# Sixty-four bytes of SBUF moved among the operand tiles of a float32 decoder trunk

## The chip, the cores and the metric

The kernel runs as one program on one core of a Trainium2 chip. The metric is the device time of one execution in microseconds (us); 842.84 us is the median of three runs of the kernel before.

## The reference

Two decoder layers over 256 tokens of width 1024, all in float32. Layer 0 mixes tokens by latent attention (MLA: low-rank query and key/value projections, rotary key), layer 1 by dilated window attention (three head groups). Each mixer is followed by a SwiGLU feed-forward net of inner width 2816 and by a gated per-layer embedding, with norms around each part:

```python
h = h + rms_norm(y, g[1])
h = h + rms_norm(swiglu(rms_norm(h, g[2]), ffn_w_in[i], ffn_w_out[i]), g[3])
h = h + (p[i] @ ple_w_proj[i]) * jax.nn.sigmoid(h @ ple_w_gate[i])
```

Here `y` is the mixer's output. Nearly all the arithmetic is the products with the weights, which are read once, 136 MB in all.

## The kernel before, in words

**Split products.** Every product with a weight is made from two-part splits in the type float32r. A value v is split into a high part (ScalarE copies v into a float32r tile, L219 for weights) and a low part (VectorE subtracts, L220). `mm3` (L291) then issues three matmuls into the same PSUM columns through `mm` (L288, the matmul itself is L289): weight high by x high, weight high by x low, weight low by x high. Each matmul is preceded by the load of its own stationary operand (a LDWEIGHTS, the engine PEld), which for one matmul runs while the matmul before it still streams. In a row such as `psin<-xh,wh 128*128 128x256` the moving operand (256 columns, 1024 bytes in each partition) is `xh`, the stationary one (128 columns, 512 bytes) is `wh`.

**Kinds of split product.** With the weight as stationary operand: x by w (`xh`, `xl`: all projections of the residual or of the attention output), u by w (`uh`, `ul`: the down projection `down`, L890), c by w (`ckvh`, `ckvl`, `cqh`, `cql`: the low-rank MLA projections) and p by w (`ph`, `pl`: the embedding, in `post_norm`). With the weight as moving operand: v of layer 1 (`v_chunk`, L1013, 384 columns, stationary `xh`, `xl`) and v of MLA (L650 to L657, 512 columns, stationary `ckvh`, `ckvl`).

**Order of the work.** The program is one written-out list for each engine. The feed-forward net goes block by block (L901 to L909): `half(f, 0)` and `half(f, 1)` are 24 matmuls x by w each into one PSUM bank, then `down(f - 3)` is 24 matmuls u by w over four banks, three matmuls at a time. The blocks f = 3 to 21 stand back to back in TensorE's list, 19 of them in each layer. In `square_matmul` (L431) and at the start of the net (L853 to L860) the outputs alternate after each three matmuls. In layer 1's mixer (L1107 to L1149) the six 24-matmul tiles of a head pair (`qk_tile`, L1007) have the attention of the pair before woven between them: scores with 64 rows, transposes, and products of probabilities with v. Eight head pairs make 1152 matmuls x by w.

**Weights.** `Stream` (L175) loads weights into three `raw` tiles of 8 KB per partition through the queue of SyncE, splits them into seven `wh` and seven `wl` tiles of 4 KB, and prepares as far ahead as free tiles allow.

**Addresses.** A pool hands out SBUF in the order in which tags are first asked for, in steps of 32 bytes; a tag with several buffers takes them side by side. The pool `main` begins with `cst` and `h`; then come, by the order of first use, `tbl` (two buffers of 32 bytes, the target of `table`, L298, that has ScalarE change its function table), `raw`, `xh`, `xl`, `wh`, `wl`, `acc` and small tiles. The pools of the stages lie behind it, each from the same byte 150464: `mla`, then `ffn` of layer 0, `dil`, and `ffn` of layer 1. All columns and chunks that the split products take begin at multiples of 512 bytes in their tiles, so one number for a tile, its address modulo 512, holds for each of its matmuls. In the program before:

| tiles | address of the first | modulo 512 |
|---|---|---|
| `tbl` (2 of 32 bytes) | 28160 | 0 |
| `raw` (3 of 8192) | 28224 | 64 |
| `xh`, `xl` (2 each of 8192) | 52800, 69184 | 64 |
| `wh`, `wl` (7 each of 4096) | 85568, 114240 | 64 |
| `ckvh`, `ckvl`, `cqh`, `cql` | 151552 to 158720 | 0 |
| `ph`, `pl`, both layers | 160704, 162752 | 448 |
| `uh`, `ul`, layer 0 (5 each of 1024) | 193024, 198144 | 0 |
| `uh`, `ul`, layer 1 | 177088, 182208 | 448 |

The `u` tiles of the two layers differ because layer 0's pool also holds the small tiles of the bias tables (L814 to L822).

Of the kernel before, what the change touches and what calls it, by code (L numbers as in the profile page):

```python
# [13 lines left out]
AF = mybir.ActivationFunctionType  # L14
# [246 lines left out]
def trunk(ctx: ExitStack, tc: tile.TileContext, tags, widths, wts, xT, pT, positions, consts,  # L261
# [7 lines left out]
    def nm(s):  # L269
        uid[0] += 1  # L270
        return f"{s}_{uid[0]}"

    def sb(tag, shape, dt=F32, bufs=1, pool=None):
        return (pool or main).tile(shape, dt, tag=tag, bufs=bufs, name=nm(tag))
# [10 lines left out]
    V, A, G, PE = nc.vector, nc.scalar, nc.gpsimd, nc.tensor  # L285
# [9 lines left out]

    px = fp = None

    def table(func, src):  # L298

        A.activation(sb("tbl", [128, 1], bufs=2), src, func)  # L300


    mla = ExitStack()
# [8 lines left out]
    def gain(i, n, k):  # L312
        c = C_G + (i * 4 + n) * 8 + k
        return cst[:, c:c + 1]


    def new_x():
        return sb("xh", [128, KT, T], F32R, bufs=2), sb("xl", [128, KT, T], F32R, bufs=2)
# [11 lines left out]

    zero = sb("zero", [128, 1], pool=mp)
    V.memset(zero, 0.0)
    table(AF.Sin, zero)

    idle = sb("ang", [128, T], pool=mp)
    V.memset(idle, 0.0)
# [13 lines left out]
    def ordered(ap):  # L350

        return ap.rearrange("p (i c) -> p c i", c=2)

    def blocks(ap):
        return ap.rearrange("p (c i) -> p c i", c=2)

    x = new_x()
    for k in range(KT):
        g = gain(0, 0, k)
        A.activation(ordered(x[0][:, k]), blocks(h[:, k]), AF.Copy, scale=g)  # L360
        V.scalar_tensor_tensor(ordered(x[1][:, k]), blocks(h[:, k]), g, ordered(x[0][:, k]).bitcast(F32),
                               op0=ALU.mult, op1=ALU.subtract)
        if k in (1, 3):
            ws.prep()
# [84 lines left out]
    def post_norm(i, n, acc, dst, proj, o0, x, g_next, sq_next, freed, ahead=0, extra=None):  # L449
# [11 lines left out]
        for k in range(KT):  # L461
# [11 lines left out]
            if k % 2 and k // 2 < len(freed):  # L473
                ws.hold(freed[k // 2], a, v)
        table(AF.Sigmoid, x[0][:, KT - 1, 0:1].bitcast(F32))
        if sq_next is not None:
            for k in range(KT):
# [112 lines left out]
    V.scalar_tensor_tensor(sin, sin, 2.0, cos, op0=ALU.mult, op1=ALU.mult)  # L590
    V.tensor_scalar(cos, kf, 1.0, None, op0=ALU.add)
    table(AF.Exp, cos[:, 0, 0:1])
    rep = sb("csr", [128, 2, 2, 128], pool=mp)
    V.tensor_copy(rep.rearrange("p a t (r f) -> p (a t) r f", f=16),
# [27 lines left out]
    for c in range(2):  # L622
        ch = ws.next("uk")
        for o in range(4):
# [12 lines left out]
            if o % 2 == 1:  # L637
                src = bu[-1].t.rearrange("p (o t) -> p o t", o=2)
# [163 lines left out]
    def sublayers(i, ot, done):  # L802
# [2 lines left out]
        ffn = ExitStack()  # L805
        fp = ffn.enter_context(tc.tile_pool(name=nm("ffn"), bufs=1))
        proj = sb("proj", [128, KT, T], pool=fp)
        pf = sb("pf", [128, 2, T], pool=fp)
        nc.gpsimd.dma_start(pf, pT[i])
        px = (sb("ph", [128, 2, T], F32R, pool=fp), sb("pl", [128, 2, T], F32R, pool=fp))  # L810
# [155 lines left out]

    mla.close()
    sublayers(0, ot, to_next)

    dil = ExitStack()  # L970
# [181 lines left out]
    def store(k):  # L1152
        nc.sync.dma_start(out[k * 128:(k + 1) * 128, :], h[:, k])

    sublayers(1, ot, store)
    assert ws.cur == len(widths)

# [72 lines left out]
```

## Time and profile before

| | |
|---|---|
| median of 3 runs | 842.84 us (842.48 to 843.18) |
| the profiled execution's own time | 842.93 us |
| its span (first to last instruction) | 841.2 us |
| TensorE busy | 827.2 us, 6780 matmuls |
| VectorE busy | 582.9 us |
| ScalarE busy | 456.7 us |
| DMA | 143.04 MB, 170 GB/s on average |

Matmuls overlap in the pipeline: a row's duration (some 0.28 us) is longer than the distance to the next start (some 0.12 us), and the distance between starts is what a matmul costs. A start in the timeline is given to 0.01 us, so distances are read over many matmuls.

### The profile page before, as it was taken

The numbers are of one execution on the slowest core, as the hardware profiler recorded it, in microseconds if no ns is written. First come the engines' busy times: TensorE is split into PE (matmuls) and PEld (weight loads), VectorE is DVE, ScalarE is ACT, GpSimd is POOL, SyncE is SP. The second block draws the span as 40 slices with busy tenths as digits, with TensorE's granted clock in tenths as the row PEclk, the third lists the DMA queues.
The fourth block names the chain that finished last, engine by engine and source line by source line (L and its number), as shares of the span: only waits on it lengthen the run. The fifth ranks groups of instructions, "written<-read, shape, count | busy, mean of one in ns | idle before, by whom it ended". The sixth has DMA issues, their size and how long they took to land.

```text
span 841.2 us, 16363 instructions
## 1 busy us (share of the span) xinstructions
PE 827.2 (98%) x6780; PEld 803.5 (96%) x6780; DVE 582.9 (69%) x1001; ACT 456.7 (54%) x782; POOL 63.8 (8%) x73
## 2 busy tenths in 40 slices
PE   8988999999999999999999999999999999999998
PEld 7976999999999999999999999999999999999997
DVE  6888478666666679695775775776578666666675
ACT  6748675444444477564554564565574444444462
POOL 3013220000000005100000000000210000000000
PEclk9999999999999999999999999999999999999999
DMA  7651336545545534755455455445426554554511
GB/s 254 212 219 51 122 102 219 202 181 201 186 172 194 200 104 151 275 175 192 147 177 182 155 170 182 163 141 198 136 82 253 194 189 168 196 188 167 197 51 51
DMA packets 23482, 143.04 MB, mean 170 GB/s; under 512 B 3071, under 2 KB 4175, under 8 KB 9200
## 3 DMA queue, kind: packets, MB, share of 16 engines
q1 hardware_dynamic: 21584, 135.98, 45.9%
q0 software_dynamic: 1824, 6.03, 2.8%
q8 instruction: 53, 0.87, 0.4%
q14 instruction: 21, 0.17, 0.1%
HBM read 140.86 MB, written 1.13 MB: 169 GB/s over the span
## 4 chain that ended last, share of the span: by engine, by line
PE 88%; DVE 4%; ACT 3%; DMA 2%; issue 1%; POOL 0%; SPq 0%; DVEq 0%; ACTq 0%
PE psin L289 40%; PE pspt L289 19%; PE psB L289 6%; PE psA L289 6%; PE psC L289 6%; PE psD L289 6%; PE psD L1092 2%; PE pspt L1075 2%; DVE wl L220 2%; DMA raw<-in_wts 1%; DMA h<-in_xT 1%; ACT mp L743 1%; ACT wh L219 1%; PE psin L771 0%; PE pspt L758 0%
## 5 line engine op out<-in xcount | busy, mean ns | idle before, releaser
L220 DVE TENSOR_TENSOR wl<-raw,wh 128x1024 fp32r<-128x1024 f32 (+1 forms) x265 | 315.6, 1197 | 160.8 <-ACT wh L219 160.0
L219 ACT ACTIVATE wh<-raw 128x1024 fp32r<-128x1024 f32 (+1 forms) x265 | 269.0, 1023 | 270.1 <-PE psin L289 115.6
L289 PE MATMUL psin<-xh,wh 128*128 128x256 f32 x768 | 220.1, 287 | 0.0
L289 PE MATMUL psin<-xh,wl 128*128 128x256 f32 x768 | 217.2, 283 | 0.0
L289 PE MATMUL psin<-xl,wh 128*128 128x256 f32 x768 | 217.1, 283 | 0.0
L289 PEld LDWEIGHTS psin<-xh,wh 128*128 128x128 f32 x768 | 146.8, 191 | 1.9 <-ACT rb L466 0.2
L289 PEld LDWEIGHTS psin<-xl,wh 128*128 128x128 f32 x768 | 146.9, 191 | 0.0
L289 PEld LDWEIGHTS psin<-xh,wl 128*128 128x128 f32 x768 | 146.9, 191 | 0.0
L289 PE MATMUL pspt<-xh,wl 128*128 128x256 f32 x440 | 124.8, 284 | 1.8 <-DVE wl L220 1.8
L289 PE MATMUL pspt<-xh,wh 128*128 128x256 f32 x440 | 125.1, 284 | 0.7 <-ACT wh L219 0.7
L289 PE MATMUL pspt<-xl,wh 128*128 128x256 f32 x440 | 124.6, 283 | 0.4 <-DVE xl L327 0.4
L289 PEld LDWEIGHTS pspt<-xh,wl 128*128 128x128 f32 x440 | 84.2, 191 | 2.4 <-DVE wl L220 2.4
L289 PEld LDWEIGHTS pspt<-xh,wh 128*128 128x128 f32 x440 | 84.2, 191 | 1.8 <-ACT wh L219 1.1
L289 PEld LDWEIGHTS pspt<-xl,wh 128*128 128x128 f32 x440 | 84.2, 191 | 0.7 <-DVE xl L327 0.6
L289 PE MATMUL psin<-wh,xh 128*128 128x384 f32 x112 | 38.2, 341 | 0.0
L289 PE MATMUL psin<-wl,xh 128*128 128x384 f32 x112 | 37.4, 334 | 0.0
L289 PE MATMUL psin<-wh,xl 128*128 128x384 f32 x112 | 37.4, 334 | 0.0
L1056 ACT ACTIVATE dpr<-dpr,st 128x512 f32<-128x512 f32 x32 | 22.9, 715 | 22.3 <-DVE st L1053 22.3
L398 POOL TENSOR_TENSOR acc<-acc,sq 128x256 f32<-128x256 f32 x24 | 25.8, 1076 | 50.5 <-ACT sq L394 30.9
L289 PE MATMUL psA<-uh,wh 128*128 128x256 f32 x88 | 24.9, 283 | 0.0
L289 PE MATMUL psA<-ul,wh 128*128 128x256 f32 x88 | 24.7, 280 | 0.0
L289 PE MATMUL psB<-ul,wh 128*128 128x256 f32 x88 | 24.6, 280 | 0.0
(355 smaller groups left out, 1702.8 us busy)
## 6 DMA issues: line engine op xcount, KB each, us to landing
raw<-in_wts SPq DMA_DIRECT2D x111, 1024.0 KB, 4.8
raw<-in_wts SPq DMA_DIRECT2D x19, 768.0 KB, 4.2
bias<-scr POOLq DMA_DIRECT2D x8, 640.0 KB, 6.5
raw<-in_wts SPq DMA_DIRECT2D x4, 384.0 KB, 5.9
out<-h SPq DMA_DIRECT2D x8, 128.0 KB, 1.7
h<-in_xT SPq DMA_DIRECT2D x2, 256.0 KB, 5.3
h<-in_xT SPq DMA_DIRECT2D x1, 512.0 KB, 7.4
raw<-in_wts SPq DMA_DIRECT2D x1, 512.0 KB, 3.7
```

Of the source, the lines that this page charges most:

```text
L219: a = self.nc.scalar.activation(h[:, :w], src, AF.Copy)
L220: v = self.nc.vector.tensor_sub(l[:, :w], src, h[:, :w].bitcast(F32))
L289: PE.matmul(o, lhsT, rhs, start=b.first(), stop=stop, skip_group_check=True)
L398: eng.tensor_tensor(self.acc, self.acc, s, op=ALU.add)
L743: A.activation(p[:, c], p[:, c], AF.Exp, bias=st[:, n:n + 1], scale=-1.0, accum_out=st[:, 2 + n:3 + n])
L1056: A.activation(p[:, t], p[:, t], AF.Exp, bias=st[:, t:t + 1], scale=-1.0, accum_out=st[:, 2 + t:3 + t])
L1075: PE.transpose(b.t[:, c * T + t * 128:c * T + (t + 1) * 128], p[:, t, n * T + c * 128:n * T + (c + 1) * 128], flip)
L1092: PE.matmul(o[s * 64:(s + 1) * 64, cols], dV[j][:, t, c], pts[s][:, 0, t] if g == 0 else pts[s][:, 1, g - 1, cols], start=g + t == 0, stop ...
```

## The change

`table` takes a target, and the first call, before any other, writes `zero` onto itself. The tag `tbl` is thereby first asked for after `new_x` (that is, behind `raw`, `xh` and `xl`, and ahead of `wh`), by a tile that nothing writes. In layer 1's feed-forward pool a tile of 64 bytes that nothing uses is put behind `proj`. No instruction is added or taken away.

```diff
-    def table(func, src):
-
-        A.activation(sb("tbl", [128, 1], bufs=2), src, func)
+    def table(func, src, to=None):
+
+        A.activation(to or sb("tbl", [128, 1], bufs=2), src, func)
+
+    def pad(n, pool):
+
+
+        sb("pad", [128, n], pool=pool)
...
-    table(AF.Sin, zero)
+    table(AF.Sin, zero, zero)
...
     x = new_x()
+    sb("tbl", [128, 1], bufs=2)
     for k in range(KT):
...
         proj = sb("proj", [128, KT, T], pool=fp)
+        if i:
+            pad(16, fp)
         pf = sb("pf", [128, 2, T], pool=fp)
```

## Rows read from the trace of the kernel before

**Rows 1.** The page: busy us (share of the span) and instructions of each engine.

```profile
PE 827.2 (98%) x6780; PEld 803.5 (96%) x6780; DVE 582.9 (69%) x1001; ACT 456.7 (54%) x782; POOL 63.8 (8%) x73
```

**Rows 2.** Busy time by stretch: us, engines, granted clock (PEclk), DMA share, GB/s.

```profile
0.00:24.00 24.00, 20.23 (x129) 18.08 (x130) 15.73 (x35) 16.06 (x31) 7.85 (x12) 1.00 0.80 265
...
133.50:299.50 166.00, 165.69 (x1409) 165.48 (x1408) 110.17 (x148) 77.37 (x105) 0.72 (x1) 1.00 0.54 190
...
347.00:593.00 246.00, 245.61 (x1961) 236.50 (x1962) 168.10 (x296) 134.85 (x214) 7.76 (x7) 1.00 0.52 176
...
634.00:803.50 169.50, 169.50 (x1419) 169.44 (x1420) 112.20 (x150) 78.50 (x106) 0.72 (x1) 1.00 0.54 192
```

**Rows 3.** Who waited for whom: us in total, times, longest us.

```profile
PE pspt L758 <- POOL mp L751: 2.3, 2, 2.1
...
ACT wh L219 <- PE psin L289: 115.6, 73, 2.5
```

**Rows 4.** Groups of matmuls by form: count, busy us, mean ns.

```profile
L289 PE MATMUL psin<-xh,wh 128*128 128x256 f32 x768 | 220.1, 287 | 0.0
...
L289 PE MATMUL psin<-wh,xh 128*128 128x384 f32 x112 | 38.2, 341 | 0.0
```

**Rows 5.** TensorE's timeline, layer 0's feed-forward block: start us, duration us, instruction.

```profile
187.28 0.28 PE L289 MATMUL psin<-xh,wh 128*128 128x256 f32 x1
...
191.60 0.29 PE L289 MATMUL psA<-uh,wh 128*128 128x256 f32 x1
...
191.96 0.28 PE L289 MATMUL psA<-uh,wh 128*128 128x256 f32 x1
...
194.34 0.28 PE L289 MATMUL pspt<-xh,wh 128*128 128x256 f32 x1
```

**Rows 6.** TensorE's timeline, layer 1's feed-forward block.

```profile
697.36 0.28 PE L289 MATMUL psin<-xh,wh 128*128 128x256 f32 x1
...
702.40 0.28 PE L289 MATMUL psA<-uh,wh 128*128 128x256 f32 x1
702.51 0.28 PE L289 MATMUL psA<-ul,wh 128*128 128x256 f32 x1
...
702.76 0.28 PE L289 MATMUL psA<-uh,wh 128*128 128x256 f32 x1
...
705.25 0.28 PE L289 MATMUL pspt<-xh,wh 128*128 128x256 f32 x1
```

**Rows 7.** TensorE's timeline, x by w with alternating banks, layer 0.

```profile
127.03 0.28 PE L289 MATMUL psin<-xh,wh 128*128 128x256 f32 x1
...
130.99 0.28 PE L289 MATMUL pspt<-xh,wh 128*128 128x256 f32 x1
```

**Rows 8.** TensorE's timeline, two runs of c by w, each after other matmuls.

```profile
30.16 0.60 PE L289 MATMUL psA<-cst,pw 128*128 128x128 f32 x4
...
31.07 0.28 PE L289 MATMUL psin<-ckvl,wh 128*128 128x256 f32 x1
...
33.00 0.28 PE L289 MATMUL pspt<-ckvh,wh 128*128 128x256 f32 x1
33.11 0.50 PE L289 MATMUL psA<-cst,accq 128*128 128x1 f32 x4
...
33.79 0.28 PE L289 MATMUL psin<-ckvh,wh 128*128 128x256 f32 x1
...
36.50 0.28 PE L289 MATMUL pspt<-ckvh,wl 128*128 128x256 f32 x1
```

**Rows 9.** TensorE's timeline, weights as moving operand: MLA's v, then layer 1's v.

```profile
38.44 0.39 PE L289 MATMUL pspt<-wh,ckvh 128*128 128x512 f32 x1
...
41.18 0.39 PE L289 MATMUL pspt<-wh,ckvh 128*128 128x512 f32 x1
...
384.34 0.33 PE L289 MATMUL psin<-wh,xh 128*128 128x384 f32 x1
...
386.42 0.33 PE L289 MATMUL psin<-wh,xh 128*128 128x384 f32 x1
```

## The prediction

> **What bounds the kernel now.** The page comes first: TensorE is busy for 98% of the span, VectorE for 69%, ScalarE for 54% [rows 1]. The stretches show that this is no average of a full and an empty part: in the two feed-forward runs and in layer 1's mixer TensorE is busy throughout at a granted clock of 1.00, that is 2.4 GHz, and its weight loads almost as long [rows 2]. Only the first 24 us differ: 129 matmuls in 24 us, with the DMA at 0.80, so there the loads set the pace. The waits say the same. The largest total of TensorE is 2.3 us, on GpSimd, and all nine that are listed come to under 10 us; the large wait stands on the other side, 115.6 us of ScalarE for TensorE to give back a weight tile [rows 3]. The time is therefore the number of matmuls times the distance between their starts, and any nanosecond off that distance shows in the end.
>
> So the view to read is the timeline, over many matmuls at a time. Take one kind of instruction, 256 moving columns against a 128-column stationary tile. In layer 0's feed-forward net 36 matmuls x by w run from 187.28 to 191.60, 120.0 ns each. The 24 matmuls u by w behind them take 191.60 to 194.34; leaving out the first three, 21 take 2.38 us, 113.3 ns each [rows 5]. In layer 1, 42 matmuls x by w take 5.04 us, again 120.0, and the 24 u by w take 2.85 us, 118.8 each [rows 6]. The u by w of the two layers are the same code with the same banks and the same weights' tiles. What differs is where the `u` tiles lie.
>
> Put the table of addresses beside that. Call the offset the moving tile's address less the stationary tile's, modulo 512. x by w has 64 - 64 = 0 and costs 120.0. Layer 0's u by w has 0 - 64 = -64 and costs 113.3. Layer 1's has 448 - 64, which is -128, and costs 118.8. c by w has -64, and its run from 31.07 costs 1.93 us for 17, 113.5 ns [rows 8].
>
> **What the change does to the offsets.** Taking the 64 bytes of `tbl` from ahead of `raw` to behind `xl` moves `raw`, `xh` and `xl` down by 64 and leaves `wh`, `wl` and all behind them in place. x by w goes from 0 to -64. The 64 bytes in layer 1's pool move `u` and `p` there from 448 to 0, so both go to -64. c by w and layer 0's u by w have -64 already. Layer 1's v has the weight as moving operand, and goes from 0 to +64, not -64. Layer 0's p by w stays at -128: there the change does not do all that its name says, but that is 48 matmuls. No instruction, transfer or wait is added, the first `table` call writes elsewhere at the same cost, and no queue is passed by anything.
>
> **The sum, against the profiled execution's 842.9 us** (0.1 us above the median).
>
> *The two feed-forward runs.* In each, 19 blocks hold 912 matmuls x by w. At 120.0 - 113.3 = 6.7 ns this is 6.1 us; I take 0.3 off, because a few of each block already stand below 120 after a change from u to x. Layer 1's u by w, some 496 in the run, gains 118.8 - 113.3 = 5.5 ns, 2.7 us. Layer 0's u by w gains only on the three costlier ones with which each of its stretches begins (0.36 us for three, against 0.34 [rows 5]), 20 ns x 19 = 0.4 us. Together 5.8 + 5.8 + 2.7 + 0.4 = 14.7 us.
>
> *The rest of x by w.* There are 4176 (psin with 768 is the largest of six groups that come three times each [rows 4]). Of these, 1152 belong to layer 1's mixer, 1824 to the runs above, and 103 to the first 24 us, where the loads set the pace and I count nothing. That leaves 1097 in the output projections, the start of the nets and the gates. These all come in short runs, and here the trace has a warning: offset -64 has two steady beats. The run of c by w that starts after the transposed norm settles at 113.5. The one that starts at 33.79, the same tiles after four one-column matmuls, stays at 2.71 / 23 = 117.8 to its end [rows 8]. Of 12 such starts of c by w behind other kinds of matmul, 9 settle at 113.3 and 3 at about 117.8. With three in four the mean gain is 0.75 x 6.7 + 0.25 x 2.2 = 5.6 ns. For the mixer this is 6.4 us, less 0.5 for some 40 starts (each loses 12 ns or so in settling) and 0.5 for matmuls that stand below 120 already: 5.4. For the other 1097 it is 6.1 less 0.5: 5.6 us.
>
> *The v of layer 1.* 384 matmuls of 384 columns cost 2.08 / 12 = 173.3 ns at offset 0. No row shows 384 columns at +64. The nearest is MLA's v, 512 columns at +64: 2.74 / 12 = 228.3 ns [rows 9]. At 2.4 GHz their columns take 160.0 and 213.3 ns, so v stands 13.3 over its columns now and MLA's v 15.0. I take 15.0: 384 x 1.7 ns = 0.7 us lost. The best end is the 6.7 ns of x by w, 2.6 us gained.
>
> Sum: 14.7 + 5.4 + 5.6 - 0.7 = 25.0 us, so 817.9.
>
> *What covers it.* The weights' preparation must keep up with a block that is 5% shorter. VectorE works 110.2 of 166.0 us in layer 0's run and the DMA engines 0.54 of the time [rows 2]; at 160 us these would be 0.69 and 0.56. ScalarE waits for TensorE rather than the reverse [rows 3], so a full set of weight tiles lies ready and no wait should take the place of the gain. Were that cover gone, the floor would be VectorE's 110 us, far away. In the mixer the softmax between scores and transposes has 5% less time under the woven matmuls; TensorE now has 0.4 us idle of 246 there [rows 2], and I price no new wait.
>
> **A rule against it.** The same instruction costs 113.3, 118.8 or 120.0 ns with nothing different but addresses [rows 5, 6]. The Trainium skill, page "TensorE: Matmul & The Clock Gate", section "Part 2: What happens when you issue a matmul", says otherwise: the moving and the stationary operand have read ports of their own, and "Loading the next tile's weights doesn't steal SBUF read bandwidth from the running matmul." By that rule no address could matter and the time would stay at 842.9; by the rows it is 817.9, and the trace does not agree with the rule.
>
> **The rivals.**
> A, the 117.8 beat in a long run. The feed-forward runs have no interruption, so each may keep for 165 us the beat that it started with. At 117.8 a run's x by w gains 2.2 ns, 1.7 us after the same deduction. Layer 0's u by w would lose: 496 x (117.8 - 114.2) = 1.8 us, where 114.2 is 2.74 / 24 [rows 5]. Layer 1's would gain 0.5. One long run at that beat costs 6.3 us (6.2 gained becomes none; in layer 1, 8.5 becomes 2.2): 824. Both at it: 831. For it: the run at 33.79 never leaves the beat in 23. Against: all 19 runs of u by w that follow x by w settle at 113.3, and the start of the long runs is behind a broadcast like the one at 30.16, which settled well.
> B, no effect: what sets 113.3 is not the offset but that u by w changes its bank after three matmuls. Then 842.9. Against: x by w with alternating banks also costs 120.0 (33 in 3.96 us [rows 7]), c by w is at 113.5 without, and layer 1's u by w changes banks as layer 0's does.
> C, slower: long x by w at -64 settles in neither beat but wanders, as layer 1's u by w does at -128, where two distances from 702.51 to 702.76 come to 125 ns each [rows 6]. At that price all through, 4073 x 5 ns is 20 us lost, and the time 863. It decides from a mean above 120.0. Against: no run at -64 wanders after its first six.
>
> **How the numbers follow.** The forecast, both long runs at the 113.3 beat, has 0.70 and gives 817.9. A has 0.23 (one run 0.15, both 0.08), B 0.05, C 0.02. The low end takes every short run at the 113.3 beat (7.1 and 6.8 in place of 5.4 and 5.6) and v's best end: 14.7 + 7.1 + 6.8 + 2.6 = 31.2, hence 812. The high end takes A in both runs, 831. B, C and mixtures beyond are left out, with about 0.1. About 0.2%, 1.7 us, can be told from no change: faster 0.93, within it 0.05 (B), slower 0.02 (C).
>
> **What would show it.** The stretch of layer 0's feed-forward run should shorten from 166.0 to about 160 us, layer 1's from 169.5 to about 161, the mixer's from 246 to about 241. In the timeline x by w should stand at 113.3 ns in the long runs, v at about 175. An x by w of 117.8 through a long run is A, 120.0 is B. TensorE waiting for VectorE's `wl` by more than the present few us would mean that the cover failed.

## The result and the profile after

The changed kernel took 822.57 us (median of 4 runs, 822.13 to 823.7) against 842.66 us for the kernel before: a ratio of 0.9764, interval 0.9753 to 0.9776. The forecast was 817.9 us, its range 812 to 831. The profiled execution of the changed kernel took 822.13 us, with a span of 820.4 us; that of before 842.93 and 841.2. So 20.8 us of span went, where 25.0 were forecast.

In a later run (experiment 10) the same changed kernel took 823.49, 828.19, 829.17 and 835.58 us: a median of 828.68, still inside the forecast's range, with one execution outside it. The kernel before stays within 841 to 844 in every run, so the spread belongs to the changed kernel; experiment 10 shows where 6 us of it come from. Of all intervals below, only that of experiment 8 leaves out executions: its two longest, which lie more than 1.5% above its shortest.

The page after, with the line of engines and the two groups that answer to [rows 1, 4]:

```profile
span 820.4 us, 16363 instructions
PE 804.0 (98%) x6780; PEld 778.5 (95%) x6780; DVE 582.3 (71%) x1001; ACT 456.4 (56%) x782; POOL 64.5 (8%) x73
...
L289 PE MATMUL psin<-xh,wh 128*128 128x256 f32 x768 | 216.1, 281 | 0.0
...
L289 PE MATMUL psin<-wh,xh 128*128 128x384 f32 x112 | 38.4, 343 | 0.0
```

TensorE makes the same 6780 matmuls in 23 us less of busy time and is still at 98%; VectorE and ScalarE do what they did. The matmuls stand closer together, and no work went.

The stretches that answer to [rows 2], with the one from 24 to 80 us added (columns as there):

```profile
24.00:80.00 56.00, 51.79 (x450) 44.46 (x448) 50.67 (x146) 38.43 (x101) 9.99 (x13) 1.00 0.46 165
133.50:293.00 159.50, 159.50 (x1410) 159.50 (x1409) 110.78 (x148) 77.28 (x105) 0.00 (x0) 1.00 0.55 196
347.00:586.00 239.00, 237.65 (x1938) 227.21 (x1937) 165.97 (x292) 133.16 (x214) 7.89 (x7) 1.00 0.52 173
624.50:784.00 159.50, 159.50 (x1410) 159.50 (x1409) 110.87 (x149) 77.68 (x105) 0.00 (x0) 1.00 0.56 198
```

The two feed-forward runs shrink from 166.0 us for 1409 matmuls and 169.5 for 1419 to 159.5 for 1410 each. The mixer has 1.35 us without TensorE where it had 0.4. For the first line, the same stretch of the kernel before, and one microsecond of it:

```profile
24.00:80.00 56.00, 52.15 (x441) 44.76 (x440) 48.69 (x137) 37.18 (x95) 10.14 (x13) 0.97 0.46 163
...
60.00:61.00 1.00, 1.00 (x10) 0.77 (x6) 0.44 (x1) 0.00 (x0) 0.83 (x1) 0.50 0.00 0
```

There the granted clock averaged 0.97: soon after TensorE's wait of 2.1 us for GpSimd [rows 3], which lies from 56 to 58 us, it stood at 0.50, that is 1.2 GHz, for some 3 us of attention scores. In the changed kernel's profile the wait is as long, and the clock stays at 1.00 throughout.

The waits that answer to [rows 3]:

```profile
PE pspt L764 <- POOL mp L757: 2.3, 2, 2.1
...
PE pspt L289 <- DVE wl L220: 1.9, 3, 1.2
...
PE pspt L1083 <- DVE dpr L1072: 1.0, 2, 0.6
PE pspt L289 <- DVE xl L332: 0.9, 1, 0.9
PE psD L289 <- POOL rdef L421: 0.6, 1, 0.6
...
PE psB L289 <- ACT xh L331: 0.2, 1, 0.2
```

The wait for weights (`wl`) stays at what it was, 1.8 us before: the cover held. The other four lines grew. The first is the mixer's transposes waiting for the softmax, 0.4 us before. The next two stand at the start of layer 0's feed-forward net, which waits for x and for its norm's factor; before:

```profile
PE pspt L289 <- DVE xl L327: 0.4, 1, 0.4
PE psD L289 <- POOL rdef L415: 0.3, 1, 0.3
```

The last is new, at the start of layer 1's mixer. It shows as little idle time, but the same 15 distances take 2.94 us after and 1.80 before; the one wait that the profile names there is for `xh`:

```profile
332.47 0.28 PE L289 MATMUL psB<-xh,wh 128*128 128x256 f32 x1
...
334.55 0.38 PE L289 MATMUL psB<-xh,wh 128*128 128x256 f32 x1 [0.21 <-ACT xh L331]
...
335.41 0.29 PE L289 MATMUL psB<-xh,wh 128*128 128x256 f32 x1
```

```profile
341.89 0.28 PE L289 MATMUL psB<-xh,wh 128*128 128x256 f32 x1
...
343.69 0.28 PE L289 MATMUL psB<-xh,wh 128*128 128x256 f32 x1
```

TensorE's timeline in both feed-forward runs, as [rows 5, 6]:

```profile
179.98 0.28 PE L289 MATMUL psA<-uh,wh 128*128 128x256 f32 x1
...
182.36 0.28 PE L289 MATMUL psin<-xh,wh 128*128 128x256 f32 x1
...
185.76 0.28 PE L289 MATMUL psin<-xh,wh 128*128 128x256 f32 x1
...
659.74 0.28 PE L289 MATMUL pspt<-xh,wh 128*128 128x256 f32 x1
...
662.80 0.28 PE L289 MATMUL psA<-uh,wh 128*128 128x256 f32 x1
...
665.52 0.28 PE L289 MATMUL psin<-xh,wh 128*128 128x256 f32 x1
```

Layer 0: 21 u by w in 2.38 us, then 30 x by w in 3.40. Layer 1: 27 x by w in 3.06, then 24 u by w in 2.72. All four are 113.3 ns. And in the mixer, as [rows 9]:

```profile
344.96 0.34 PE L289 MATMUL pspt<-wh,xh 128*128 128x384 f32 x1
...
347.04 0.34 PE L289 MATMUL pspt<-wh,xh 128*128 128x384 f32 x1
...
351.21 0.28 PE L289 MATMUL psin<-xh,wh 128*128 128x256 f32 x1
...
353.91 0.28 PE L289 MATMUL psin<-xh,wl 128*128 128x256 f32 x1
...
355.58 0.28 PE L289 MATMUL psin<-xh,wh 128*128 128x256 f32 x1
...
357.85 0.28 PE L289 MATMUL psin<-xh,wl 128*128 128x256 f32 x1
```

v: 12 in 2.08 us, 173.3 ns as before, though its offset is now +64. The x by w tile behind v: 23 in 2.70 us, 117.4. The next tile, behind scores: 20 in 2.27, 113.5. Two tiles of the same code and the same offset keep two different beats.

Where the time went, from the starts of all matmuls in program order, one profile against the other (the distance to the next start counts with a matmul, and so does a wait in it):

| part | forecast, us | measured, us |
|---|---|---|
| two feed-forward runs | −14.7 | −14.4 (layer 0 −6.05, layer 1 −8.33) |
| output projections, rest of the nets, gates | −5.6 | −3.6 |
| mixer, x by w | −5.4 | −3.2 |
| mixer, v | +0.7 | 0.0 |
| mixer, other matmuls (transposes) | 0 | +1.3 |
| MLA (the clock above) | 0 | −1.6 |
| the first 24 us, matmuls other than x by w (loads set the pace there) | 0 | +0.7 |
| sum | −25.0 | −20.8 |

A feed-forward run is taken here, and below, from the first matmul of block 3 to the first of the last four chunks of the down projection, 1344 distances: 158.47 and 160.75 us before, 152.42 and 152.42 after. At 113.3 ns that is 152.3, at 117.8 it is 158.3.

Two rows hold waits that are no matter of the beat. In the row of the output projections and nets, the start of layer 0's net waits 0.8 us longer than before (`xl` 0.49, `rdef` 0.31, both read from the starts). In the mixer's x by w, the start costs 1.2 us (above), and 0.8 us lie ahead of the mixer's first transpose. It waits for the softmax (`dpr`), and in the kernel before it followed at once:

```profile
365.39 0.30 PE L1083 MATMUL pspt<-cst,dpr 128*128 128x128 f32 x1 [0.64 <-DVE dpr L1072]
```

Without these waits the two rows are −4.4 and −5.2.

The 1.6 us are not the change's: a third profile, of the changed kernel again, has that dip to 0.97 too.

### The profile page after: what moved, and what is told of

It reads as the page before. It is cut to its first block, busy times and chain, and to the rows that moved or that the text cites. A ratio compares the mean times of both kernels' runs of the same rounds, so it can differ in the third digit from the quotient of the medians.

```text
span 820.4 us, 16363 instructions
## 1 busy us (share of the span) xinstructions
PE 804.0 (98%) x6780; PEld 778.5 (95%) x6780; DVE 582.3 (71%) x1001; ACT 456.4 (56%) x782; POOL 64.5 (8%) x73
## 4 chain that ended last, share of the span: by engine, by line
PE 80%; DVE 10%; ACT 6%; issue 2%; POOL 1%; DMA 1%; SPq 0%; DVEq 0%; ACTq 0%
PE psin L289 34%; PE pspt L289 17%; PE psC L289 6%; PE psA L289 6%; PE psB L289 6%; PE psD L289 5%; DVE wl L220 3%; PE psD L1100 2%; PE pspt L1083 2%; ACT dpr L1064 1%; ACT wh L219 1%; DVE dpr L1072 1%; POOL h L948 1%; DVE xl L332 1%; DVE h L477 1%
## 5 line engine op out<-in xcount | busy, mean ns | idle before, releaser
L289 PE MATMUL psin<-xh,wh 128*128 128x256 f32 x768 | 216.1, 281 | 0.0
L289 PE MATMUL psin<-xl,wh 128*128 128x256 f32 x768 | 213.2, 278 | 0.0
L289 PE MATMUL psin<-xh,wl 128*128 128x256 f32 x768 | 213.2, 278 | 0.0
L289 PEld LDWEIGHTS psin<-xh,wh 128*128 128x128 f32 x768 | 144.5, 188 | 1.9 <-ACT rb L472 0.2
L289 PEld LDWEIGHTS psin<-xl,wh 128*128 128x128 f32 x768 | 144.4, 188 | 0.2
L289 PE MATMUL pspt<-xh,wl 128*128 128x256 f32 x440 | 122.2, 278 | 1.9 <-DVE wl L220 1.9
L289 PE MATMUL pspt<-xh,wh 128*128 128x256 f32 x440 | 122.5, 278 | 0.6 <-ACT wh L219 0.6
L289 PE MATMUL pspt<-xl,wh 128*128 128x256 f32 x440 | 122.0, 277 | 0.9 <-DVE xl L332 0.9
L289 PE MATMUL psB<-uh,wh 128*128 128x256 f32 x88 | 24.4, 277 | 0.0
L289 PE MATMUL psD<-uh,wh 128*128 128x256 f32 x88 | 24.4, 277 | 0.0
```

What stands on the lines that cost most here:

```text
L289: PE.matmul(o, lhsT, rhs, start=b.first(), stop=stop, skip_group_check=True)
```

## The experiments

The main theory is the prediction's: the moving tile's address less the stationary tile's, modulo 512, decides the distance between matmuls. Against it stand that a tile's own place modulo 512 does, that only the size or only the sign of the offset counts, and, for the two beats at one offset, different accounts of what chooses between them. Each experiment's text names its own theories. A "run" below is a stretch of split products not interrupted by another kind of matmul; its settled beat is the mean of its last distances.

**1. The weights moved instead of x.** From the kernel before:

```diff
     x = new_x()
+    sb("pad", [128, 16])
```

x stays at 64 and the weights go to 128. x by w and layer 0's u by w are at −64, layer 1's u by w at −128.

> The kernel before, with 64 unused bytes between xl and wh and nothing else: xh and xl stay at 64, wh, wl and all behind them move up by 64 (wh at 128). Offsets (moving less stationary, modulo 512): x by w -64, u by w still -64 in layer 0 and -128 in layer 1. Theory O (the offset between the two operands decides): x by w at 113.3 or 117.8 ns, 825 us (the 20 us of the change less the 2.8 us of layer 1's u by w). Rival R (the moving tile's own place decides, fast at 0 modulo 512, as x and layer 0's u both are after the change): x by w stays at 120.0 ns, layer 0's u by w at 64 goes to 120 and layer 1's at 0 to 113.3: 843 us.

Measured: 826.3 us (2 runs), ratio 0.9809, interval 0.9776 to 0.9843. TensorE's timeline in layer 0's net:

```profile
198.95 0.28 PE L289 MATMUL psin<-xh,wh 128*128 128x256 f32 x1
...
203.03 0.28 PE L289 MATMUL psin<-xh,wh 128*128 128x256 f32 x1
...
203.37 0.28 PE L289 MATMUL psA<-uh,wh 128*128 128x256 f32 x1
```

36 x by w in 4.08 us, 113.3 ns, with x where it always was. The feed-forward runs take 152.42 and 157.13 us; the second has the u tiles at −128. The new wait in the mixer is here too (other matmuls +1.3 us).

**2. Both at 0.** The placeholder goes from behind `xl` to behind `wl`, and the padding of layer 1's pool goes. x and w both lie at 0; nothing else of the change is undone.

```diff
     x = new_x()
-    sb("tbl", [128, 1], bufs=2)
     for k in range(KT):
...
     ws.top_up(3)
+    sb("tbl", [128, 1], bufs=2)
...
-        if i:
-            pad(16, fp)
```

> The 64 bytes of tbl are put behind wl, so that x and w both lie at 0; no pad in layer 1. Offsets: x by w 0, layer 0's u by w and c by w 0, layer 1's u by w -64. Theory O: x by w at 120.0 ns, layer 0's u by w 120 (+3 us), layer 1's 113.3 (-2.8 us): 843 us. Rival R: x by w at 113.3 or 117.8 ns since x lies at 0: about 825 us.

Measured: 843.59 us, the time before. The timeline in layer 0's net:

```profile
187.30 0.28 PE L289 MATMUL psin<-xh,wh 128*128 128x256 f32 x1
...
192.70 0.28 PE L289 MATMUL psA<-uh,wh 128*128 128x256 f32 x1
...
195.10 0.28 PE L289 MATMUL psD<-uh,wl 128*128 128x256 f32 x1
```

45 x by w in 5.40 us and 20 u by w in 2.40, both 120.0. Layer 0's u by w, at −64 and 113.3 in the kernel before, goes up to 120.0 with its tiles left where they were: its weights moved under it. With the first experiment this settles that the offset counts and not either tile's own place. The `raw` tiles, which the change moves as well, lie here as in the changed kernel and in experiment 1 as before it, so they are not the cause. The mixer's other matmuls are back too (−0.1 us), so the new wait belongs to the closer matmuls.

**3. The other sign.** From the kernel before, w at 0 and x at +64:

```diff
     x = new_x()
+    sb("pad", [128, 112])
```

> 448 unused bytes between xl and wh: x at 64, w at 0, x by w at +64; u and c keep their offsets, layer 1's v goes to -64. Theory Os (the sign counts, the stationary tile must be the one that lies ahead): x by w at 118 to 122 ns, 838 to 846 us; v of layer 1 below 173.3 ns, down to 166.6. Rival Od (only the distance counts): x by w at 113.3 or 117.8 ns, 825 us, v at 173.3 as at +64.

Measured: 838.19 us. Neither account fits. x by w nearly everywhere keeps the second beat:

```profile
186.77 0.28 PE L289 MATMUL psin<-xh,wh 128*128 128x256 f32 x1
...
191.01 0.28 PE L289 MATMUL psin<-xh,wh 128*128 128x256 f32 x1
```

36 in 4.24 us, 117.8. But most of layer 1's output projection and the start of its feed-forward run are at 113.3. So +64 has the same two beats as −64, and what differed in this execution is how often each was taken. In the mixer the offset decides it: all 14 tiles of x by w behind scores are at 117.8 here, and all 14 are at 113.3 in the changed kernel. v, at −64 here, costs +0.2 us in all: 384 columns take 173 at 0, at +64 and at −64.

**4. Without the padding of layer 1's pool.** The changed kernel less one edit:

```diff
         proj = sb("proj", [128, KT, T], pool=fp)
-        if i:
-            pad(16, fp)
```

> The change without the 64 bytes in layer 1's feed-forward pool. Theory O: layer 1's u by w stays at 118.8 ns, x by w as after the change: 2.8 us slower than the changed kernel, 825.4 us, and the same offsets as the run that moves the weights up by 64, so the same time as that within 1.5 us. Rival R: the same here, but then the two runs differ by 18 us.

Measured: 827.6 us (2 runs), ratio 0.9825, interval 0.9786 to 0.9863. The feed-forward runs take 152.42 and 157.14 us, against 152.42 twice. Experiment 1 has the same offsets and lies 1.3 us away, as expected. The padding is worth 4.7 us in layer 1's run. Of these u by w at −128 costs 2.4 by itself. The other 2.3 are lost by the x by w behind its irregular beat, which is at −64: it settles block by block in turn at 117.8 and at 113.3 (ten and nine of 19 blocks, in both experiments).

**5 and 6. A map of offsets.** Each weight tile is made 4128 bytes long in place of 4096, so that the seven tiles of `wh` and of `wl` lie at seven different offsets under one x. The sixth also moves x by 224 bytes.

```diff
-        h = self.pool.tile([128, 1024], F32R, tag="wh", bufs=self.NHL, name=f"wh{i}")
-        l = self.pool.tile([128, 1024], F32R, tag="wl", bufs=self.NHL, name=f"wl{i}")
+        h = self.pool.tile([128, 1032], F32R, tag="wh", bufs=self.NHL, name=f"wh{i}")
+        if i == 0:
+            self.pool.tile([128, 72], F32, tag="pad", bufs=1, name="pad")
+        l = self.pool.tile([128, 1032], F32R, tag="wl", bufs=self.NHL, name=f"wl{i}")
```

> The kernel before with weight tiles of 4128 instead of 4096 bytes (32 unused at the end of each), and 288 bytes between wh and wl, so that the seven buffers lie at 64, 96, ... 256 modulo 512 and x by w has, tile by tile, the offsets 0, -32, -64, -96, -128, -160, -192. A run of 24 matmuls against one tile then shows the beat of one offset. Theory O: 120.0 ns at 0, 113.3 or 117.8 at -64, about 119 at -128, and something of its own at the others; in all 830 to 843 us. If the distance had to be exact to 64 bytes, the odd multiples of 32 would show 120 throughout. An offset with 113.3 and no second beat would be better than -64. Rival: the offset works through the whole stage and not tile by tile, then all tiles show one beat.

> As the run with the offsets 0 to -192, but x lies 224 bytes higher, so that x by w has the offsets 224, 192, 160, 128, 96, 64, 32. Theory O: about 117.7 ns at 64, as in the run at +64, and each of the others its own beat between 113 and 122; if the offsets fold at 256, 224 to 128 answer to -288 to -384, that is far from any seen so far, and may be free of the second read altogether (113.3 throughout, better than the changed kernel's mean of some 115).

Measured: 839.26 and 837.33 us. Mixed offsets give nearly all the gain away. The settled beat of the stretches of 20 and more at one offset (the mean of their last nine distances, rounded), from both profiles:

| offset | stretches at each beat, ns |
|---|---|
| 0 | 120: 29 of 29 |
| −160 | 120: 23 of 23 |
| +160 | 117 to 120, mixed (28) |
| ±96 | 120: 11 of 12 at +96; 117 to 118 at −96 (8) |
| ±32 | 116 to 118 at +32 (29); 118 to 119 at −32 (33) |
| +128 | 119 (4) |
| +224 | 118 to 119 (23) |
| −64 | 113: 18, 118: 10 |
| +64 | 113: 9, 118: 18 |
| −192 | 113: 14, 118: 9 |
| +192 | 113: 23, 118: 2 |

Four offsets reach 113, and all four also hold 118. No other does.

The table also shows that 512 is more than is needed: offsets that differ by 256 behave alike. −160 and +96 stand at 120, −32 and +224 at 118 to 119, and −96 lies in the span of +160. The single distances agree as well: a stretch at −32 (experiment 5) and one at +224 (experiment 6) both end on 120, 117, 122, 118, 117, 121, 116, 116, 120 ns, and one at −160 (experiment 5) and one at +96 (experiment 6) both on 118, 121, 117, 125, 116, 123, 118, 121, 117. So −64 goes with +192 and +64 with −192.

**7 and 8. The changed kernel at +192 and at −192.** x, u and p are moved by padding; the seventh:

```diff
+    sb("padx", [128, 64])
     x = new_x()
     sb("tbl", [128, 1], bufs=2)
+    sb("pady", [128, 64])
...
-        if i:
-            pad(16, fp)
+        pad(80, fp)
...
             tb = sb("tb", [HEADS, len(TABLES) * 256], pool=fp)
+            sb("pad2", [128, 112], pool=fp)
```

The eighth has 96 and 32 floats around `new_x` and 112 in `pad`.

> The changed kernel with x and u moved so that x by w and u by w have the offset +192 in both layers (p by w too; c by w stays at -64). In the run of tiles at changing offsets, 23 of 25 tiles at 192 settled at 113.3 and 2 at 118, against 18 of 25 at -64. Theory M (each offset has its own share of starts that settle at 113.3): a larger share than at -64, so faster than the changed kernel by 2 to 5 us, 818 to 820 us. Rival H (the share there came from the tile before, at another offset, and not from 192 itself): the same share of about half, 821 to 824 us.

> The same with the offset -192, where 14 of 22 tiles settled at 113 and 8 at 118. Theory M: about as the changed kernel, 821 to 825 us; layer 1's v at +192 may leave its 173.3 ns. Rival H: the share changes with what precedes, anywhere from 818 to 832 us.

Measured: at +192 828.42, 829.03, 833.78 and 834.92 us, ratio 0.9878, interval 0.9844 to 0.9912; at −192 824.33, 832.56, 838.22 and 838.8 us, ratio 0.9829, interval 0.9772 to 0.9886. The map's 23 of 25 at +192 does not carry over: with one offset throughout, 63 stretches of 20 and more of one kind settle at 113 and 59 at 118, layer 1's feed-forward run among the latter (158.38 us). At −192 both long runs are at 113.3 in the profiled execution, that of 824.33. In the mixer the choice goes by the offset modulo 256 and by what stands ahead: behind scores all 14 tiles are at 113.3 at +192, as at −64, and all 14 at 117.8 at −192, as at +64; behind v all seven are at 117.8 in all four. Neither kernel is better than −64, and single executions of one kernel are 6 to 14 us apart, which would follow if the choice between the two beats were made anew in every execution; the next runs look at that.

**9 and 10. The transposes one step later, beside the changed kernel again.** In the ninth the softmax of a head pair gets one more woven tile of x by w before its transposes:

```diff
-        return [lambda: d_score(j, 0), lambda: d_score(j, 1), lambda: None, lambda: d_trans(j, 0),
+        return [lambda: d_score(j, 0), lambda: d_score(j, 1), lambda: None, lambda: None, lambda: d_trans(j, 0),
```

> The changed kernel with one more empty step ahead of the transposes in layer 1's mixer, so that 24 more matmuls stand between the scores and the transposes of a pair. Theory W (the transposes wait for the softmax since the matmuls over it have become shorter): the 1.3 us by which the other matmuls of the mixer grew are gone, 821.2 us. Rival: the growth lies elsewhere (weight loads, banks), then 822.5 us or more, since the products with v come later.

> The changed kernel once more, as the measure for the three others on the same chip. Theory: each start of a run settles at 113.3 or 117.8 by its phase, which is not the same in every execution: the profile shows other runs at 117.8 than the first profile of this kernel (where the output projection of layer 0 and the gate of layer 1 had it), and times spread by 1 to 2 us around 822.6. Rival: the beat is fixed by the program, then the same runs show 117.8.

Measured: 821.08, 825.39, 827.94 and 833.25 us with later transposes, ratio 0.9811, interval 0.9755 to 0.9866; 823.49, 828.19, 829.17 and 835.58 for the changed kernel, ratio 0.9837, interval 0.9782 to 0.9891. The intervals overlap, so the whole time does not tell them apart. The mixer does. The group of the transposes in the kernel before, then in the changed kernel:

```profile
L1075 PE MATMUL pspt<-cst,dpr 128*128 128x128 f32 x128 | 17.1, 274 | 0.4 <-DVE dpr L1064 0.4
```

```profile
L1083 PE MATMUL pspt<-cst,dpr 128*128 128x128 f32 x128 | 18.1, 276 | 1.4 <-DVE dpr L1072 1.0
```

And with the transposes one step later, the same group and the mixer's stretch:

```profile
L1083 PE MATMUL pspt<-cst,dpr 128*128 128x128 f32 x128 | 16.7, 272 | 0.0
```

```profile
347.00:585.00 238.00, 238.00 (x1936) 228.66 (x1936) 165.76 (x294) 133.64 (x213) 8.04 (x7) 1.00 0.53 182
```

The idle time before the transposes goes from 1.4 us to none, and TensorE is busy for all of the 238 us. Against the kernel before, the mixer gains 4.5 us up to the first matmul of the output projection, against 1.9 in the first profile of the changed kernel and 1.6 in the tenth. Of the 2.9 between ninth and tenth, 2.0 are matmuls other than split products. The last attention runs in another order with the added step and takes part of it back: at its end 2.0 of the 2.9 are left.

The tenth is worth as much for its own profile. Layer 0's feed-forward run takes 152.42 us again; layer 1's takes 158.38:

```profile
659.82 0.28 PE L289 MATMUL pspt<-xh,wh 128*128 128x256 f32 x1
...
665.12 0.28 PE L289 MATMUL psA<-uh,wh 128*128 128x256 f32 x1
```

45 in 5.30 us, 117.8, and so for all matmuls of the run. In the ninth's profile it is layer 0's run that takes 158.38. The same program takes either beat at the run's start and keeps it to its end: this is rival A of the prediction, for one long run. The ninth and tenth ran on the same chip, and up to the mixer they are the same program, so the chip does not choose the beat alone; whether it has a part is not shown (the first four executions lie within 1.6 us, the tenth's four within 12).

**11 and 12. Can the start be made to choose 113.3?** Both add one pair of weight tiles of its own place in the feed-forward pool, for the first tile of the long run and the gate's first chunk. In the eleventh it lies at offset 0 under x, in the twelfth at −64 like all others. Both also have the later transposes.

```diff
+        if i in self.own:
+            h, l = self.own.pop(i)(i)
+        else:
...
+        sb("pada", [128, 16], pool=fp)
+
+        def own(i, fp=fp):
+            return [fp.tile([128, 1024], F32R, tag="own" + t, bufs=1, name=f"w{t}{i}") for t in "hl"]
...
+        ws.own[wg[1]] = ws.own[ga[0]] = own
```

> The changed kernel with the later transposes, and in each layer's feed-forward pool one weight tile more (high and low part) at 0 modulo 512. It takes the weights of half(3, 0), the first tile of the long run, and of the gate's first chunk, so that these 24 (24) matmuls x by w run at offset 0 and all that follow at -64. Theory L (a run that comes to -64 out of the 120.0 ns beat of offset 0 settles at 113.3 every time, as all 19 runs of u by w of layer 0 did before): both feed-forward runs at 113.3 in every execution, the four tiles cost 0.6 us, the mixer keeps the gain of the later transposes: 819 us, all executions within 2.5 us of each other. Rival N (what precedes a run does not fix its beat): executions spread over 6 to 13 us, as those of the changed kernel did.

> The same kernel with the additional weight tile at 64 modulo 512, so that its matmuls have the offset -64 like all others: the additional buffer without the start at 0. Theory L: the long runs settle by their start's phase, at 113.3 or 117.8, so executions lie at 818, 824 and 831 us, whichever runs are at 117.8; the median is above that of the kernel that starts at 0. Rival B (the additional buffer is what helps): the same times as the kernel that starts at 0.

Measured: 833.52, 833.78, 834.44 and 835.59 us with the first tile at 0, ratio 0.9899, interval 0.9886 to 0.9913; 820.54, 826.41, 827.03, 828.34 and 831.88 with it at −64, ratio 0.9829, interval 0.9806 to 0.9852. The start of the long run in layer 0, eleventh kernel (its matmul is line 293):

```profile
133.07 0.28 PE L293 MATMUL psin<-xl,wh 128*128 128x256 f32 x1
...
135.71 0.28 PE L293 MATMUL psin<-xh,wl 128*128 128x256 f32 x1
135.82 0.28 PE L293 MATMUL psin<-xh,wh 128*128 128x256 f32 x1
...
138.53 0.28 PE L293 MATMUL psin<-xh,wl 128*128 128x256 f32 x1
```

22 in 2.64 us, 120.0; then, at −64 again, 23 in 2.71, 117.8, and so on to the end. Both long runs take 158.42 us. So theory L is wrong: a leading tile at 0 goes with a steadier choice, 2 us between executions in place of 11, but it goes to the slower beat. In the kernel before, u by w behind x by w at 0 settled at 113.3 in all 19 runs of layer 0, and in experiment 2 in 18 of 19 runs of layer 1; there the moving tile changed its place, here the stationary one. That the moving tile must be the one to change, out of the beat of 120.0, fits these, and was not tried by itself. Out of 117.8 it does not help: in experiment 3 layer 0's u by w, at −64, stays at 117.8 behind x by w at +64 in 18 of 19 runs. No version here is surely faster than the changed kernel: the best single executions lie between 820.5 and 822 us.

## Why the prediction came out as it did

**The cause held.** "The time is therefore the number of matmuls times the distance between their starts", and the offset sets the distance: experiments 1 and 2 move one side each and the distance follows the difference. Rival B falls with them, and with it the rule quoted from the Trainium skill, page "TensorE: Matmul & The Clock Gate", section "Part 2: What happens when you issue a matmul". Experiment 2 and the changed kernel differ by addresses alone and lie 21 us apart; the traces do not agree with the forecast of no effect that the prediction drew from that rule. Which accesses of the two operands get in each other's way, no run shows.

**The feed-forward runs, 14.7 us, held:** 14.4 measured, and 14.8 with the last four chunks of layer 1's down projection, which the forecast's 496 u by w take in and the table has one row lower. Both runs took the forecast's beat in the first profile, which is luck as far as the next profile tells.

**The waits were priced at nothing and cost some 4 us.** This is the largest miss. The softmax's wait took 1.3 us among the transposes and 0.8 ahead of the first; the start of the mixer 1.2 (for x) and the start of layer 0's net 0.8 (for x and the norm's factor). "I price no new wait" named the softmax's smaller cover and then took TensorE's 0.4 us of idle time for slack. It was the opposite: a wait of 0.4 us is a chain already on the path, and part of what the woven matmuls gave up came back as waiting. Experiment 9 removes this one. The waits at the two starts are in no term of the prediction; "any nanosecond off that distance shows in the end" did not hold there, where TensorE comes close behind the engines that make x.

**"The other 1097", 5.6 us, and the mixer's x by w, 5.4, came out at 3.6 and 3.2,** in good part by these waits. In the mixer 2.0 of the missing 2.2 us are waits: its share at 113.3 is 0.69 of the matmuls (all tiles behind scores, half of those behind transposes, and the start; none behind v), close to the forecast's three in four. With 0.69 the prediction's own sum gives 5.1, less 2.0 is 3.1. Among the other 1097 the share is near one half: the first output projection, the second gate and the start of layer 1's net stand at 117.8, the first gate, most of the second output projection and the start of layer 0's net at 113.3. One half in place of three in four is 1.2 us, the wait 0.8. The 3.6 hold 0.4 us of u by w (above), so 0.4 us more are not traced. The 12 starts of c by w stood for other neighbours, and what stands ahead goes with the beat.

**v, +0.7 us, was 0.0.** 384 columns cost 173.3 at 0 and at +64. The nearest row, 512 columns, did not carry over.

**Nothing for MLA and the first 24 us:** −1.6 and +0.7, the first from the granted clock alone. That is luck: without it the span would have shrunk by 19.2 us.

By the rows of the table these add up: +0.3 +2.0 +2.2 +1.3 −0.7 −1.6 +0.7 = 4.2 us, the distance from 25.0 to 20.8.

**Rival A was nearer than its chance of 0.23 says.** It was priced at 6.3 us for one long run; layer 1's net, with the last four chunks of its down projection, gained 8.7 us in the first profile and 2.5 in the tenth, so 6.3. But the prediction took A for a property of the changed kernel, one way or the other. It is a property of each execution: the profiled one with both runs at 113.3 took 822.13 us, the one with layer 1's at 117.8 has a span 7.0 us longer, and with neither it would be some 6 us more again, 835, an estimate from the same two runs (158.38 less 152.42). The longest of the eight executions, 835.58, fits that, but no profile shows which beats it had. Rival C, a mean above 120.0, was not seen in any long run at −64.

What stays open is what chooses the beat at a run's start. In the mixer it goes with the offset and with what stands ahead, and repeats from profile to profile; the long runs start alike each time, behind a broadcast, and still differ.

## What to carry to other kernels

Where TensorE is the bound, measure the distance between the starts of its matmuls over dozens of them, for each kind, before anything else; where the same shape has two distances, put the addresses of both operands beside them. Keep one offset for all split products of a run, since one kind at a bad offset also slows the good ones behind it. And a short wait that already stands on the path is a warning, not slack: what is woven around it can't be shortened for free. Before a faster TensorE is priced, look at each place where it comes close behind the engine that makes its operand, also where no wait shows yet.

## What was not expected of the hardware

- The distance between two matmuls of 256 columns follows the moving address less the stationary address, and modulo 256 is enough for all that was seen: 120 ns at 0 and at −160 and +96, 113.3 or 117.8 at ±64 and ±192, around 118 to 119 at −32, +128 and +224, mixed between 117 and 120 at +160.
- Two steady beats at one offset, 113.3 and 117.8, are both kept without a change for more than 1300 matmuls (152.4 or 158.4 us of one long run), and the same program takes now one, now the other: 822 to 836 us.
- Which of the two beats a tile takes goes with what stands ahead of it: at −64 and +192 all 14 tiles behind scores took 113.3 and all seven behind v 117.8.
- A single tile at offset 0 ahead of a long run went with 117.8 in both profiled long runs and narrowed the executions to 833.5 to 835.6 us.
- Matmuls of 384 columns with the weight moving cost 173.3 ns at offsets 0 and +64 alike.
